# RWKV-7 streaming encoder on one core: pieces, loads and writes around the recurrence moved, and the gate's products around a norm put in a fixed order

## The chip, the cores and the metric

The kernel runs on one core of a Trainium2 chip. A core has a matrix engine (TensorE, PE in the profile; its weight loads are PEld), VectorE (DVE), ScalarE (ACT), GpSimd (POOL) and SyncE (SP), each with an instruction queue of its own that runs in order, and 16 DMA engines. The metric is the device time of one execution in microseconds; the median of the runs counts, lower is better.

## The reference, cut to what matters

A trunk of two residual layers on an input of 1024 tokens by 1024 columns, each followed by a SwiGLU FFN, and a norm at the end. The first layer is a mixer that the change does not touch. The second is RWKV-7 time mixing; its state is a recurrence over the tokens, per head of 64 columns (16 heads):

```python
def step(state, inp):
    r_t, w_t, k_t, v_t, a_t, b_t = inp
    sa = jnp.einsum('bhvk,bhk->bhv', state, a_t)
    state = (state * w_t[:, :, None, :] + sa[..., None] * b_t[:, :, None, :]
             + v_t[..., None] * k_t[:, :, None, :])
    return state, jnp.einsum('bhvk,bhk->bhv', state, r_t)
...
y = ((y - mean) * lax.rsqrt(var + GN_EPS)).reshape(bsz, seq, d)
y = y * ln_w.astype(f32) + ln_b.astype(f32)
bonus = jnp.sum(rh * kh * r_k.astype(f32), axis=-1, keepdims=True) * vh
y = (y + bonus.reshape(bsz, seq, d)).astype(h.dtype)
return (y * g) @ w_o, v_first
```

The gate is `g = sigmoid(xg @ g1) @ g2` with 160 columns between. `rms_norm` stands before each layer and each FFN.

## The kernel before, in words

Tokens are worked in two halves of 512 (half 0, half A; half 1, half B). A product in float32 is made of three products of parts, high by high, high by low, low by high (`mm3`, lines 408 to 411; a dense block of eight `mm3` is 24 matmuls of 128x128 by 128x512). Weights come by DMA issued on ACT's queue into `raw` and are split into `whi` (ACT) and `wlo` (DVE) by `split` (158 to 160). Other DMAs are issued on SP's queue. A scheduler lays out every engine's order when the kernel is compiled, by priority and by its own estimate of times; `tc.high_priority` moves what it holds ahead, `tc.issue_after` puts instructions behind another on their queue, and `tc.manual_schedule` keeps the written order for the engines it names. At run time each queue runs in that order.

The stages that the change touches, in order of time:

- `project(h)` (1202): the projections of the time mixing for one half. The recurrence is done in chunks of 64 tokens; inside a chunk a triangular system is solved with an inverse, which `invert` (1432) forms in 31 steps on DVE, for four pairs of heads at a time. So there are two inverses per half, the first beside the products for v, the second after it; both use the same buffer `xi` (cleared by POOL, line 1437) and `iat` (loaded at 1273 to 1280). At its end an inverse is copied (1450) and written to `xi_d` by three DMAs (1452, 1454).
- `recur(h)` (1469): eight chunks. `load(c)` (1504) loads `ar` (with `bk`), `XT` (the inverse, from `xi_d`) and `uv`. The first loads, then `stream` (the residual stream H of the other half), then chunk 1's loads are written in that order (1738 to 1744). `gram` makes the Gram products of a chunk from `ar`, `flip_bk` transposes, `below` and `below2` complete the inverse with `XT`, `own` and the rest of `burst` (1589) carry the state. Each product of the recurrence is chained behind the last on PE (`ordered`). `drive` interleaves the recurrence with dense FFN products, with the recurrence at high priority.
- `post(jj)` (1671) works on the output of two chunks: loads of `gch` and `vch`, the product with `bon` on POOL (1685), statistics (1690), a power on POOL (`rsqrt`, 1701 and 414), the norm (1703 on), and `turn_out`, which transposes it on PE and writes `y_d`. It is a generator: `between()` (1666) takes its next step at six places of a burst, behind the last DVE instruction of the recurrence's chain. A post is started after an odd burst and runs in the even one that follows; the last one runs after the eighth burst.
- After the recurrence of half 0 its `y` is read from `y_d` and split into `ahi`, `alo` (`open_act`, 481), and `beside(1, ...)` (994) runs the output projection and the first FFN blocks of half A beside `side`, the token mixes of half B, the low-rank products and the gate (`gate`, 1153: 24 matmuls for `g1`, 24 for `g1b`). At step 8 it calls `norm_a` (2033): row sums of squares by four small matmuls (444), `norm_rows` (mean, POOL's power, a diagonal, a broadcast matmul at 457), and `norm_split` (466), which makes `hn` and its parts for the FFN's products.

Buffers are placed by pools as on a stack. Before, the buffer of H for the first recurrence lies where `xi` of `project` lay.

Of the kernel before, what the change touches and what calls it, by code (L numbers as in the profile page):

```python
# [16 lines left out]
P = 128  # L17
# [28 lines left out]
def tile_trunk(  # L46
# [392 lines left out]

    def norm_bcast(acc):  # L440

        st = auxt()
        for j in range(4):
            pe.matmul(st[:, j : j + 1], acc[:, j * P : (j + 1) * P], onesd, start=True, stop=True)
        return norm_rows(st[:, 0:4])

# [16 lines left out]
    def act_tiles(pool_, n=HT):  # L463
        return [pool_.tile([P, KT, n], F32R, tag=t, name=t) for t in ("ahi", "alo")]

# [528 lines left out]
    def beside(h, gen, weights, parts, at=()):  # L994

        side, lowrank, gate = parts
        at = {} if not at else dict([at])
        due, done = 0.0, 0

        def step():  # L1000
            nonlocal done
            next(side, None)
            done += 1

        for i, weight in enumerate(weights):
            if i == LOWRANK_AT[h]:
                while done < KT:
                    step()
                lowrank()
            if i in at:  # L1010
                at[i]()
            if i == GATE_AT[h]:
                while done < 2 * KT:
                    step()
                gate()
            w = 0.0
            while w < weight - 0.001:
                w += next(gen)
                if i >= MIX_AT[h]:
                    due += 1.0  # L1020
                    while due >= 1.0 and (done < 2 * KT or i >= LOWRANK_AT[h]) and (done < 3 * KT or i >= GATE_AT[h]):
                        due -= 1.0
                        step()
        exhaust(gen)
        exhaust(side)
# [87 lines left out]
    def project_gate(h, hn1, kp, xlp, ring):  # L1113
# [38 lines left out]

        def gate():
            for nm, n in (("g1", P), ("g1b", 96)):
                wg = take((nm, h))
                o = mmt()
                dense2(o[:n], *wg, xs, n)
                t = nt.tile([P, HT], F32, tag="nsq", bufs=2, name="gt")
# [273 lines left out]
    def invert(h, p0, iat, tmp):  # L1432
# [18 lines left out]
        to = xi_d[h][p0 : p0 + 4].rearrange("p r c q i x -> (p r c) q i x")  # L1451
        sp.dma_start(to[:, 0, :, 0:64], x2[0:64].rearrange("s i a j -> s i (a j)"))
        for q in range(2):
            sp.dma_start(to[:, q, :, 64 - 32 * q : 96 - 32 * q], x2[64:128, :, 0, :])  # L1454

# [13 lines left out]
    def recur(h, wp, stream, ratio):  # L1469
# [34 lines left out]
        def load(c):  # L1504
            ab = wt("ar", 2, [P, 2, 8, 2, 64])
            sp.dma_start(ab, ab_d[h][c])
            ar, bk = ab[:, 0], ab[:, 1]
            XT = wt("XT", 2, [P, 8, 96])
            for r in range(2):
                sp.dma_start(XT[rows[r]], xi_d[h][:, r ^ (c % 2), c].rearrange("p q i x -> (q i) p x"))  # L1510
            uv = wt("uv", 2, [P, 2, 8, 64])
            vs = v_d[h][c * 64 : c * 64 + 64]
            sp.dma_start(uv[64:128, 0], vs[:, 0])
            loaded[0] = sp.dma_start(uv[0:64, 1], vs[:, 1])
            gt = wt("gt", 2, [P, 8, 2, P])
            C[c] = (ar, bk, uv, gt, XT)

# [71 lines left out]
        def burst(c, bkt, w1):  # L1589
# [53 lines left out]
            if more:  # L1643
                bkt = flip_bk(c + 1)
                if turned or pieces:
                    for _ in pieces.pop():
                        pass
                    turned.pop()()
# [14 lines left out]

        turned, chain, pieces = [], [None], []

        def between():
            if pieces:
                with tc.issue_after(chain[0]):
                    next(pieces[0], None)

        def post(jj):
            ysb = [ypair.pop(0) for _ in range(2)]
            j = h * 4 + jj
# [13 lines left out]
            yield  # L1687
            for r in range(2):
                for p in range(8):
                    dve.bn_stats(out=st[:, r, p, :], in_=ysb[r][:, p, :])  # L1690
                yield
# [8 lines left out]
            dve.tensor_scalar(out=var, in0=var, scalar1=1.0 / 64, scalar2=GN_EPS, op0=ALU.mult, op1=ALU.add)  # L1700
            rsqrt(var)
            yield
            dve.scalar_tensor_tensor(out=mean, in0=mean, scalar=-0.5, in1=var, op0=ALU.mult, op1=ALU.mult)
# [37 lines left out]
        with tc.issue_after(loaded[0].ins):  # L1741
            stream_loaded = stream()
        with tc.issue_after(stream_loaded):
            load(1)
        yield START * ratio
# [8 lines left out]
        for c in range(8):  # L1754
            bkt, w1 = yield from burst(c, bkt, w1)
            yield BURST / 2
            if c % 2 == 1:
                pieces[:] = [post(c // 2)]
                next(pieces[0])
            yield BURST / 2  # L1760
        for _ in pieces[0]:
# [226 lines left out]

    ps_es = open_psum("psm0", MIXED)
    hb_pool, hb_es = open_pool(name="hb1", bufs=1, side="left")  # L1990
    wp, wp_es = open_pool(name="wp0", bufs=1, side="left")
# [8 lines left out]
    y, y_es = open_pool(name="y0", bufs=1, side="left")  # L2000
    ys = open_act(("y", 0), y)
    between.append(with_first(0))
# [29 lines left out]

    def norm_a():
        hnA.extend(norm_split(0, C_FFN + 8, y, n_d[1], norm_bcast(sums)))

    beside(1, blocks(), [1] * 8 + weights_of(G1A[0]), parts, (8, norm_a))
    for e in (f_es, y_es, hb_es, ps_es):
        e.close()
# [72 lines left out]
```

## Time and profile before

| | us |
|---|---|
| median of 3 runs | 2402.95 |
| lowest, highest | 2401.16, 2412.61 |
| the profiled execution | 2407.23 |
| its span, first to last instruction | 2405.5 |
| PE busy in the span | 2319.2 |
| DVE busy | 1464.6 |
| ACT busy | 946.9 |
| POOL busy | 171.2 |

The granted clock of PE over the span was 0.986. The page gives busy time by engine, then the span in 40 slices, then DMA queues, the chain of work that ended last, and the costliest groups. In the page's slices PE stands at 9 tenths or more in nearly all; 8 stands in the first and the last slice and in those that begin at about 960, 1020, 1140 and 1620 us. A row of the timeline gives start, duration, engine, line, operation, the tiles as output<-inputs, shapes, a count, and in brackets the idle time of the engine before it and what ended it. An engine with a q behind its name (SPq, ACTq) is its sequencer, which issues DMAs.

The page's DMA part lists two queues that carry the kernel's transfers: one with 195.33 MB (27.3% of the 16 engines' span) and one with 150.25 MB (20.9%).

### The profile page before, as it was taken

The numbers are of one execution on the slowest core, as the hardware profiler recorded it, in microseconds if no ns is written. First come the engines' busy times: TensorE is split into PE (matmuls) and PEld (weight loads), VectorE is DVE, ScalarE is ACT, GpSimd is POOL, SyncE is SP. The second block draws the span as 40 slices with busy tenths as digits, with TensorE's granted clock in tenths as the row PEclk, the third lists the DMA queues.
The fourth block names the chain that finished last, engine by engine and source line by source line (L and its number), as shares of the span: only waits on it lengthen the run. The fifth ranks groups of instructions, "written<-read, shape, count | busy, mean of one in ns | idle before, by whom it ended". The sixth has DMA issues, their size and how long they took to land.

```text
span 2405.5 us, 37578 instructions
## 1 busy us (share of the span) xinstructions
PE 2319.2 (96%) x15315; PEld 1893.9 (79%) x15315; DVE 1464.6 (61%) x2312; ACT 946.9 (39%) x1467; POOL 171.2 (7%) x195
## 2 busy tenths in 40 slices
PE   8999999999999999889899999998999999999998
PEld 6888888888888788667777777777778788888886
DVE  6445775665568858656768958765664546444443
ACT  6233444444224755323336665423332225222223
POOL 0200000000000022101100022101010001000001
PEclk9999999999999999999999999999999999999999
DMA  5114472334765565775445475776534433433231
GB/s 181 53 49 145 149 198 83 129 99 146 283 226 191 156 173 140 209 218 157 130 135 165 148 199 147 193 222 177 163 89 149 123 88 119 127 96 97 79 114 44
DMA packets 446157, 347.97 MB, mean 145 GB/s; under 512 B 119776, under 2 KB 393312, under 8 KB 443680
## 3 DMA queue, kind: packets, MB, share of 16 engines
q10 hardware_dynamic: 266048, 195.33, 27.3%
q1 hardware_dynamic: 179936, 150.25, 20.9%
q8 instruction: 120, 1.97, 0.4%
q14 instruction: 53, 0.43, 0.1%
HBM read 266.47 MB, written 79.04 MB: 144 GB/s over the span
## 4 chain that ended last, share of the span: by engine, by line
PE 77%; DVE 9%; DMA 6%; issue 2%; ACT 2%; SPq 2%; POOL 2%; ACTq 0%; POOLq 0%; DVEq 0%
PE mm L409 17%; PE mm L410 17%; PE mm L411 17%; PE mm L740 5%; PE mm L742 5%; PE mm L741 5%; PE sm L1491 3%; DMA ar<-ab_d 1%; DVE wlo L160 1%; DMA raw<-y_d 1%; SPq L1454 1%; DVE it L1443 1%; DMA raw<-in_ffn_w_down_dram 1%; PE mm L590 1%; PE mm L591 1%
## 5 line engine op out<-in xcount | busy, mean ns | idle before, releaser
L409 PE MATMUL mm<-ahi,whi 128*128 128x512 f32 x1376 | 541.0, 394 | 4.2 <-ACT ahi L159 2.6
L410 PE MATMUL mm<-alo,whi 128*128 128x512 f32 x1376 | 542.0, 394 | 0.9 <-DVE alo L160 0.9
L411 PE MATMUL mm<-ahi,wlo 128*128 128x512 f32 x1376 | 540.6, 393 | 1.6 <-DVE wlo L160 1.6
L159 ACT ACTIVATE whi<-raw 128x1024 fp32r<-128x1024 f32 (+2 forms) x284 | 286.3, 1014 | 507.1 <-PE mm L410 367.7
L160 DVE TENSOR_TENSOR wlo<-raw,whi 128x1024 fp32r<-128x1024 f32 (+2 forms) x284 | 337.6, 1192 | 233.6 <-ACT whi L159 212.4
L409 PEld LDWEIGHTS mm<-ahi,whi 128*128 128x128 f32 x1376 | 259.0, 188 | 62.9 <-issue 3.5
L411 PEld LDWEIGHTS mm<-ahi,wlo 128*128 128x128 f32 x1376 | 259.2, 188 | 58.5 <-DVE wlo L160 2.9
L410 PEld LDWEIGHTS mm<-alo,whi 128*128 128x128 f32 x1376 | 259.3, 188 | 57.4 <-issue 2.9
L503 DVE TENSOR_TENSOR h<-h,mm 128x512 f32<-128x512 f32 x276 | 185.9, 684 | 156.1 <-PE mm L411 152.9
L411 PE MATMUL mm<-hidhi,wdlo 128*128 128x512 f32 x304 | 119.6, 394 | 0.0
L409 PE MATMUL mm<-hidhi,wdhi 128*128 128x512 f32 x304 | 117.2, 392 | 2.3 <-ACT sg L957 2.3
L410 PE MATMUL mm<-hidlo,wdhi 128*128 128x512 f32 x304 | 118.6, 390 | 0.0
L740 PE MATMUL mm<-ahi,whi 128*128 128x512 f32 x296 | 115.6, 390 | 0.0
L741 PE MATMUL mm<-alo,whi 128*128 128x512 f32 x296 | 115.2, 389 | 0.0
L742 PE MATMUL mm<-ahi,wlo 128*128 128x512 f32 x296 | 113.6, 389 | 0.0
L965 DVE TENSOR_TENSOR sg<-sg,mm 128x512 f32<-128x512 f32 x52 | 35.7, 686 | 125.7 <-PE mm L411 125.7
L159 ACT ACTIVATE wdhi<-raw 128x1024 fp32r<-128x1024 f32 x42 | 43.6, 1058 | 169.0 <-PE mm L410 126.9
L160 DVE TENSOR_TENSOR wdlo<-raw,wdhi 128x1024 fp32r<-128x1024 f32 x42 | 51.4, 1223 | 30.9 <-ACT wdhi L159 29.2
L409 PEld LDWEIGHTS mm<-hidhi,wdhi 128*128 128x128 f32 x304 | 57.2, 188 | 14.7 <-ACT sg L957 2.7
L411 PEld LDWEIGHTS mm<-hidhi,wdlo 128*128 128x128 f32 x304 | 57.2, 188 | 12.2 <-issue 0.5
L410 PEld LDWEIGHTS mm<-hidlo,wdhi 128*128 128x128 f32 x304 | 57.2, 188 | 12.0 <-issue 0.2
L409 PE MATMUL mm<-xhi,whi 128*128 128x512 f32 (+1 forms) x160 | 64.9, 406 | 0.0
(392 smaller groups left out, 4226.2 us busy)
## 6 DMA issues: line engine op xcount, KB each, us to landing
raw<-in_ffn_w_down_dram ACTq DMA_DIRECT2D x88, 512.0 KB
raw<-in_ffn_w_gate_dram ACTq DMA_DIRECT2D x74, 512.0 KB
raw<-in_ffn_w_up_dram ACTq DMA_DIRECT2D x74, 512.0 KB
hid_d<-hid SPq DMA_DIRECT2D x36, 512.0 KB
ar<-ab_d SPq DMA_DIRECT2D x16, 1024.0 KB
hd<-hid_d SPq DMA_DIRECT2D x26, 512.0 KB
raw<-in_ab_w_in_dram ACTq DMA_DIRECT2D x16, 512.0 KB
raw<-in_ab_w_out_dram ACTq DMA_DIRECT2D x16, 512.0 KB
```

Source lines behind the costliest of these rows:

```text
L159: act.activation(hi, src, AF.Copy)
L160: (eng or dve).tensor_tensor(out=lo, in0=src, in1=hi.bitcast(F32), op=ALU.subtract)
L409: pe.matmul(o, whi, xhi, start=first, stop=False)
L410: pe.matmul(o, whi, xlo, start=False, stop=False)
L411: newest[0] = pe.matmul(o, wlo, xhi, start=False, stop=last).ins
L503: dve.tensor_tensor(out=H[h][:, m, :], in0=H[h][:, m, :], in1=o, op=ALU.add)
L590: pe.matmul(ops[j], xhi[:, k, sl], whi[:, kk], start=(k == 0), stop=False)
L740: pe.matmul(o, wh[:, k, :], x[0][:, k, :], start=st, stop=False, skip_group_check=True)
L741: pe.matmul(o, wh[:, k, :], x[1][:, k, :], start=False, stop=False, skip_group_check=True)
L742: pe.matmul(o, wl[:, k, :], x[0][:, k, :], start=False, stop=k == 3, skip_group_check=True)
L965: dve.tensor_tensor(out=s, in0=s, in1=o, op=ALU.mult)
L1491: i = f(*args, **kw)
```

## The change

Six things are done.

1. `row_sums` is split from `norm_bcast`. `norm_a` now gets the gate from `beside` and runs it in a fixed order on PE: the 24 products of `g1`, the row sums, 12 products of `g1b`, the broadcast, the other 12. `norm_rows` and `norm_split` stand at high priority.
2. The three writes of an inverse are issued by POOL and not by SP.
3. `load_x` loads `XT` by itself: for chunk 0 behind the stream of H and ahead of chunk 1's loads, else with the chunk as before. `XT` is allocated after `gt`.
4. A `post` is started before the odd burst, with its loads; in the odd burst one step of it is taken (`open_`), the rest in the even burst. It takes a chunk's output from `ypair` only when it needs it.
5. Behind the power of `post` one more `yield` stands, so that one place of a burst lies between it and the instruction that reads it.
6. `ahi` of half 0's `y` has a pool of its own, `yhi`, opened ahead of H's buffer.

```diff
@@ -437,12 +437,16 @@
 
         return acc, add
 
-    def norm_bcast(acc):
+    def row_sums(acc):
 
         st = auxt()
         for j in range(4):
             pe.matmul(st[:, j : j + 1], acc[:, j * P : (j + 1) * P], onesd, start=True, stop=True)
-        return norm_rows(st[:, 0:4])
+        return st[:, 0:4]
+
+    def norm_bcast(acc):
+
+        return norm_rows(row_sums(acc))
 
     def norm_rows(ms, scale=1.0):
 
@@ -461,7 +465,7 @@
         return norm_bcast(norm_sums(h))
 
     def act_tiles(pool_, n=HT):
-        return [pool_.tile([P, KT, n], F32R, tag=t, name=t) for t in ("ahi", "alo")]
+        return [(pool_[i] if type(pool_) is tuple else pool_).tile([P, KT, n], F32R, tag=t, name=t) for i, t in enumerate(("ahi", "alo"))]
 
     def norm_split(h, c0, pool_, spill=None, b=None):
 
@@ -1007,12 +1011,13 @@
                 while done < KT:
                     step()
                 lowrank()
-            if i in at:
-                at[i]()
             if i == GATE_AT[h]:
                 while done < 2 * KT:
                     step()
-                gate()
+                if i in at:
+                    at[i](gate)
+                else:
+                    gate()
             w = 0.0
             while w < weight - 0.001:
                 w += next(gen)
@@ -1150,11 +1155,11 @@
 
         xs = []
 
-        def gate():
+        def gate(between=()):
             for nm, n in (("g1", P), ("g1b", 96)):
                 wg = take((nm, h))
                 o = mmt()
-                dense2(o[:n], *wg, xs, n)
+                dense2(o[:n], *wg, xs, n, between if nm == "g1b" else ())
                 t = nt.tile([P, HT], F32, tag="nsq", bufs=2, name="gt")
                 act.activation(t[:n], o[:n], AF.Tanh, scale=0.5)
                 sigm(t[:n], t[:n])
@@ -1449,9 +1454,9 @@
             yield
         dve.tensor_copy(x2[:, :, 0, :], xi.rearrange("p i c -> p c i"))
         to = xi_d[h][p0 : p0 + 4].rearrange("p r c q i x -> (p r c) q i x")
-        sp.dma_start(to[:, 0, :, 0:64], x2[0:64].rearrange("s i a j -> s i (a j)"))
+        pool.dma_start(to[:, 0, :, 0:64], x2[0:64].rearrange("s i a j -> s i (a j)"))
         for q in range(2):
-            sp.dma_start(to[:, q, :, 64 - 32 * q : 96 - 32 * q], x2[64:128, :, 0, :])
+            pool.dma_start(to[:, q, :, 64 - 32 * q : 96 - 32 * q], x2[64:128, :, 0, :])
 
 
 
@@ -1505,15 +1510,17 @@
             ab = wt("ar", 2, [P, 2, 8, 2, 64])
             sp.dma_start(ab, ab_d[h][c])
             ar, bk = ab[:, 0], ab[:, 1]
-            XT = wt("XT", 2, [P, 8, 96])
-            for r in range(2):
-                sp.dma_start(XT[rows[r]], xi_d[h][:, r ^ (c % 2), c].rearrange("p q i x -> (q i) p x"))
             uv = wt("uv", 2, [P, 2, 8, 64])
             vs = v_d[h][c * 64 : c * 64 + 64]
             sp.dma_start(uv[64:128, 0], vs[:, 0])
             loaded[0] = sp.dma_start(uv[0:64, 1], vs[:, 1])
-            gt = wt("gt", 2, [P, 8, 2, P])
-            C[c] = (ar, bk, uv, gt, XT)
+            C[c] = (ar, bk, uv, wt("gt", 2, [P, 8, 2, P]), wt("XT", 2, [P, 8, 96]))
+            if c:
+                load_x(c)
+
+        def load_x(c):
+            for r in range(2):
+                loaded[0] = sp.dma_start(C[c][4][rows[r]], xi_d[h][:, r ^ (c % 2), c].rearrange("p q i x -> (q i) p x"))
 
         def gram(c, q):
             ar, bk, _, gt, _ = C[c]
@@ -1642,9 +1649,8 @@
             yield 0.1
             if more:
                 bkt = flip_bk(c + 1)
-                if turned or pieces:
-                    for _ in pieces.pop():
-                        pass
+                if c and c % 2 == 0:
+                    exhaust(pieces.pop())
                     turned.pop()()
                 if c < 6:
                     load(c + 2)
@@ -1661,15 +1667,16 @@
                 yield 0.1
             return bkt, w1
 
-        turned, chain, pieces = [], [None], []
+        turned, chain, pieces, open_ = [], [None], [], [0]
 
         def between():
-            if pieces:
+            if pieces and open_[0]:
+                open_[0] -= 1
                 with tc.issue_after(chain[0]):
                     next(pieces[0], None)
 
         def post(jj):
-            ysb = [ypair.pop(0) for _ in range(2)]
+            ysb = []
             j = h * 4 + jj
             gch = wt("gch", 1, [P, 8, P])
             vch = wt("vch", 1, [P, 2, 8, 64])
@@ -1686,6 +1693,7 @@
             st = wt("st", 1, [P, 2, 8, 6])
             yield
             for r in range(2):
+                ysb.append(ypair.pop(0))
                 for p in range(8):
                     dve.bn_stats(out=st[:, r, p, :], in_=ysb[r][:, p, :])
                 yield
@@ -1699,6 +1707,7 @@
             dve.tensor_tensor(out=var, in0=var, in1=dm, op=ALU.add)
             dve.tensor_scalar(out=var, in0=var, scalar1=1.0 / 64, scalar2=GN_EPS, op0=ALU.mult, op1=ALU.add)
             rsqrt(var)
+            yield
             yield
             dve.scalar_tensor_tensor(out=mean, in0=mean, scalar=-0.5, in1=var, op0=ALU.mult, op1=ALU.mult)
             vb, mb = (bc(t[:, 0:8].unsqueeze(2), [P, 8, 64]) for t in (var, mean))
@@ -1741,6 +1750,8 @@
         with tc.issue_after(loaded[0].ins):
             stream_loaded = stream()
         with tc.issue_after(stream_loaded):
+            load_x(0)
+        with tc.issue_after(loaded[0].ins):
             load(1)
         yield START * ratio
         last.append(newest[0])
@@ -1752,12 +1763,12 @@
         w1 = below(0)
         yield 2.0
         for c in range(8):
-            bkt, w1 = yield from burst(c, bkt, w1)
-            yield BURST / 2
             if c % 2 == 1:
                 pieces[:] = [post(c // 2)]
                 next(pieces[0])
-            yield BURST / 2
+            open_[0] = (99, 1)[c % 2]
+            bkt, w1 = yield from burst(c, bkt, w1)
+            yield BURST
         for _ in pieces[0]:
             yield 0.3
         turned.pop()()
@@ -1987,6 +1998,7 @@
 
 
     ps_es = open_psum("psm0", MIXED)
+    yhi, yhi_es = open_pool(name="y0hi", bufs=1, side="left")
     hb_pool, hb_es = open_pool(name="hb1", bufs=1, side="left")
     wp, wp_es = open_pool(name="wp0", bufs=1, side="left")
     f, f_es = open_pool(name="ffn1", bufs=1, side="right")
@@ -1998,7 +2010,7 @@
     drive(ffn(0, 1, nxt["hn"], f, D0P[:3], nd=2), recur(0, wp, in_pieces(hb_pool, 1, h_d[1, 0]), 6.2), 6.2)
     wp_es.close()
     y, y_es = open_pool(name="y0", bufs=1, side="left")
-    ys = open_act(("y", 0), y)
+    ys = open_act(("y", 0), (yhi, y))
     between.append(with_first(0))
     drive(ffn(0, 1, nxt["hn"], f, D0P[3:], nd=2))
     drive(steps_b)
@@ -2030,11 +2042,23 @@
         yield from out_proj(0, ys, sums_a)
         yield from ffn(1, 0, hnA, f, G1A[0], nd=2, after=spill_a)
 
-    def norm_a():
-        hnA.extend(norm_split(0, C_FFN + 8, y, n_d[1], norm_bcast(sums)))
+    def norm_a(gate):
+        got = []
+        between = [lambda: None] * KT
+        between[0] = lambda: got.append(row_sums(sums))
+
+        def rows_():
+            with tc.high_priority(offset=AHEAD):
+                got.append(norm_rows(got[0]))
+
+        between[4] = rows_
+        with tc.manual_schedule(engines={mybir.EngineType.PE}):
+            gate(between)
+        with tc.high_priority(offset=AHEAD):
+            hnA.extend(norm_split(0, C_FFN + 8, (yhi, y), n_d[1], got[1]))
 
     beside(1, blocks(), [1] * 8 + weights_of(G1A[0]), parts, (8, norm_a))
-    for e in (f_es, y_es, hb_es, ps_es):
+    for e in (f_es, y_es, hb_es, yhi_es, ps_es):
         e.close()
     ps_es = open_psum("psp1", PROJ)
     project(1, hn1, kp, ring, keep, early("n1", "act2", nxt["a_es"]))
```

## The prediction, made before the result

> **What bounds the kernel.** I read the page first, then the windows (busy time by stretch), then the timeline of single engines where the windows show TensorE (PE) idle.
>
> ```profile
> PE 2319.2 (96%) x15315; PEld 1893.9 (79%) x15315; DVE 1464.6 (61%) x2312; ACT 946.9 (39%) x1467; POOL 171.2 (7%) x195
> ```
>
> PE is busy for 2319.2 of 2405.5 us. At most 86.3 us of idle time can go, and what a halved clock costs after it. The change takes out no product that weighs, so the question is which of these idle stretches it touches.
>
> ```profile
> core 0: us, PE busy (x) PEld busy (x) DVE busy (x) ACT busy (x) POOL busy (x), PEclk, DMA share, GB/s
> 960.00:1040.00 80.00, 72.09 (x344) 57.61 (x343) 59.44 (x119) 32.27 (x46) 8.27 (x4) 1.00 0.68 185
> 1040.00:1060.00 20.00, 9.97 (x214) 8.42 (x212) 5.77 (x10) 2.01 (x6) 0.00 (x0) 0.74 1.03 290
> 1080.00:1240.00 160.00, 149.66 (x2485) 119.72 (x2484) 106.90 (x247) 54.24 (x108) 20.18 (x8) 0.97 0.47 140
> 1600.00:1620.00 20.00, 17.54 (x302) 14.10 (x305) 8.39 (x14) 2.60 (x6) 0.00 (x0) 0.91 0.92 285
> 1640.00:1660.00 20.00, 16.12 (x314) 13.12 (x308) 12.46 (x33) 6.73 (x12) 1.90 (x1) 0.91 0.50 141
> 1660.00:1740.00 80.00, 76.78 (x1380) 61.73 (x1376) 53.29 (x112) 27.69 (x57) 10.59 (x4) 1.00 0.58 165
> 1740.00:1760.00 20.00, 17.20 (x326) 13.66 (x326) 16.49 (x47) 8.89 (x18) 2.90 (x1) 0.91 0.31 87
> ```
>
> Ten of 20 us are idle where the first recurrence starts (1040 to 1060), and the clock stands at 0.74 there. The first recurrence (1080 to 1240) loses 160 - 149.66 = 10.3 us, the second (1640 to 1760) 3.9 + 3.2 + 2.8 = 9.9 us. Those are the places that the change works on, with the stretch around 1335 (below).
>
> **The start of a recurrence.** What held PE at 1042.9 is read in SP's queue:
>
> ```profile
> 1035.34 1.09 DVE L1450 COPY xi<-xi 128x1024 f32<-128x1024 f32 x1
> 1036.50 0.61 SPq L1452 DMA_DIRECT2D xi_d<-xi  x1
> 1037.16 7.18 SPq L1454 DMA_DIRECT2D xi_d<-xi  x2
> 1044.43 2.68 SPq L1506 DMA_DIRECT2D ar<-ab_d  x1
> 1048.93 1.27 SPq L1510 DMA_DIRECT2D XT<-xi_d  x2
> 1052.41 3.69 PE L1491 MATMUL sm<-ar 64*64 64x128 f32 x64 [9.50 <-DMA ar<-ab_d]
> 1056.03 1.51 PE L1491 MATMUL sm<-ident,ar 128*128 128x128 f32 x8
> 1057.46 0.45 PE L1491 MATMUL sm<-XT,gt 32*32 32x32 f32 x32
> ```
>
> The load of `ar` stands behind the three writes of the inverse, though it reads nothing of them; its Gram products stand at the head of PE's queue and hold everything behind. The change sends the writes to POOL's queue and puts the loads of `XT` behind the stream of H, so `ar` can be issued as soon as SP is done with the last rows of v. The 9.50 us go. What is late next is `XT`, for the products `below`. From the end of the copy (1035.34 + 1.09 = 1036.43) to the issue of the `XT` load (1048.93) the writes took 12.5 us; for the load's landing I take 4 us (between 0 and the 8.5 us from 1048.93 to 1057.46). PE, starting its Gram products at 1042.9, comes to `below` after 3.69 + 1.51 us, at 1048.1. So it waits until 1052.9, 4.8 us: the gain is 9.5 - 4.8 = **4.7 us**, and the half clock stays. Behind the waiting `XT` load on SP stand the loads of chunk 1; they were issued at about this time before, so I put no price on them.
>
> The second half in the same way:
>
> ```profile
> 1584.38 1.09 DVE L1450 COPY xi<-xi 128x1024 f32<-128x1024 f32 x1
> 1597.20 1.27 SPq L1510 DMA_DIRECT2D XT<-xi_d  x2
> 1602.32 3.04 PE L1491 MATMUL sm<-ar 64*64 64x128 f32 x64 [2.67 <-DMA ar<-ab_d]
> 1610.34 0.45 PE L1491 MATMUL sm<-XT,gt 32*32 32x32 f32 x32
> ```
>
> Here the writes took 1597.20 - 1585.47 = 11.7 us; with 4 us for the load `XT` is there at 1601.2, and `below` would stand at 1610.34 - 2.67 = 1607.7. No wait takes the place: **2.7 us**, and half of what the clock of 0.91 over 20 us costs (1.8 us), **0.9**.
>
> **The writes on POOL.** No transfer in this trace is issued by POOL, so their price is unknown. The low end is SP's 12.5 us, less the queue. The high end comes from how far POOL is stretched beside other work:
>
> ```profile
> 912.04 0.74 POOL L1374 TENSOR_SCALAR ar<-kkn 128x8 f32<-128x8 f32 x1 [0.96 <-ACT kkn L1369]
> 961.89 4.16 POOL L1374 TENSOR_SCALAR ar<-kkn 128x8 f32<-128x8 f32 x1 [3.20 <-ACT kkn L1369]
> ```
>
> The same instruction takes 0.74 or 4.16 us, 5.6 times as long. Against SP's issue of 7.84 us (1036.50 to 1044.34) that is 44 us, and with the 4.6 us from there to 1048.93 some 49 us. I take SP's 12.5 us: the same packets go through the same 16 DMA engines, and it is the only row of these transfers.
>
> The Trainium skill, page "SBUF — State Buffer", section "SBUF: two separate sides", speaks against this edit: descriptors of a transfer issued by GpSimd are written by GpSimd's own cores, and these are locked out while VectorE runs an operation that takes both ports; it names 620 ns that became 3100 ns. By that factor of five the writes would take 62 us as an estimate, and the sum below would end near 2481 us. No run here shows such a transfer yet; the two rows of POOL agree in kind.
>
> The first inverse of each half is moved too:
>
> ```profile
> 979.89 11.28 SPq L1454 DMA_DIRECT2D xi_d<-xi  x2
> 991.27 2.42 SPq L1274 DMA_DIRECT2D iat<-at_d  x1
> 998.85 1.82 POOL L1437 MEMSET xi<- 128x2048 f32 x1 [30.89 <-DMA v_d<-sg]
> 999.85 1.32 DVE L1281 TENSOR_SCALAR iat<-iat 128x32 f32<-128x32 f32 x1 [4.03 <-DMA iat<-n_d]
> ```
>
> The second load of `iat` no longer stands 11.28 us behind the writes. But the second inverse also needs the buffer `xi`, which is free only when the writes have read it (the clearing at 998.85), so I put this at nothing. On POOL the clearing stands behind the writes; it waits for them anyway, and POOL has no other work from 968 to 998.85.
>
> **The pieces beside the recurrence.** `post` starts one burst earlier (loads, the product with `bon`, half of the statistics), and there is an empty step behind POOL's power, whose result VectorE (DVE) now asks for one step later.
>
> ```profile
> L414 POOL TENSOR_TENSOR var<-var,small x8: 2899/2902/3871, 1104.1 to 1788.5; 128x16 f32<-128x16 f32 x8
>   POOL var L414: 6.2, 4
> 1194.01 0.18 DVE L1703 SCALAR_TENSOR_TENSOR mean<-mean,var 128x16 f32<-128x16 f32 x1 [2.38 <-POOL var L414]
> 1196.30 0.66 PE L1491 MATMUL sm<-ident,ar 128*128 128x128 f32 x4 [1.94 <-DVE gt L1530]
> 1198.18 0.45 PE L1491 MATMUL sm<-ident,ysb 128*128 128x128 f32 x1 [1.23 <-DVE ysb L1714]
> ```
>
> The power takes 2.9 us; line 1703, which reads it, kept DVE idle for 6.2 us in 4 cases (second line: what line 1703 waited for). In the case shown DVE's 2.38 us cost PE 1.94 + 1.23 us, so I take PE's gain as large as DVE's: **6.2 us**. The bounds are 0 (PE has dense products beside it) and the 20.2 us of both recurrences. Of the clock (0.97 over 160 us and 0.91 over 20 us: 4.8 + 1.8 us) I take a quarter, **1.6 us**. The last piece of each half is shorter by its loads and half its statistics; in half 0 its end leads to the loads of `y_d`, where I take **1 us**. The loads of `gch` and `vch` now stand ahead of chunk c+2's on SP; those have a whole chunk of slack.
>
> `ahi` of `y` gets its own place (`yhi`), which moves H's buffer off that of the inverse: the stream need not wait for the writes. It is what lets `XT` stand behind the stream at no price.
>
> **The second norm of half A.**
>
> ```profile
> 1326.69 0.69 DVE L2025 TENSOR_TENSOR nacc<-nacc,nsq 128x512 f32<-128x512 f32 x1
> 1328.45 0.39 PE L411 MATMUL mm<-xhi,wlo 128*128 128x512 f32 x1
> 1332.13 0.95 PE L444 MATMUL aux<-small,nacc 128*128 128x1 f32 x8
> 1335.67 1.10 PE L457 MATMUL aux<-ndg,ones 128*128 128x512 f32 x2 [0.44 <-DVE ndg L453]
> 1339.39 0.97 PE L409 MATMUL mm<-ahi,whi 128*128 128x512 f32 x3 [2.62 <-ACT ahi L159]
> 1341.25 0.79 PE L410 MATMUL mm<-alo,whi 128*128 128x512 f32 x1 [0.90 <-DVE alo L160]
> ```
>
> The gate's 24th product starts at 1328.45; the row sums came behind the 39th (1332.13), the broadcast behind the 48th (1335.67), and PE then stood for 2.62 and 0.90 us. The sums are ready at 1327.4, so row sums at 1328.7 need not wait. From row sums to broadcast it took 3.5 us; 12 products of 0.23 us and the sums fill 3.6. So the broadcast comes at 1332.3, 3.4 us earlier, and the other 12 products lie beside `hn` and `ahi` (3.7 us from broadcast to first product). I take **3.3 us** and nothing of the clock, since DVE's pace over the eight blocks (0.7 us each for `hn` and for `alo`) then sets it. If `nacc` comes late in the new order, PE waits for it with everything behind: that would cost at most what is gained.
>
> **Sum.** 4.7 + 3.6 + 7.8 + 1.0 + 3.3 = 20.4 us. Against it stands that the compiler lays out all queues anew, and a dense stretch can then meet a late weight. At 1640 to 1660 PE loses 3.9 us, as much as I take off: **4 us**. So 16.4 us from the profiled execution's 2407.23 us: 2390.8. The median shown (2402.95) is 4.3 us under it: **2387 us**, 0.7% faster.
>
> **Rivals.** A measurement of this kernel tells some 0.5%, 12 us, from no change.
>
> *POOL writes slowly (slower).* One mechanism: `XT` comes late at `below(0)`, and PE stands with the dense products behind it. With t for the writes the waits are t - 7.7 us (half 0, before 9.5) and t - 18.2 us (half 1, before 2.7). At t = 30, between the ends, 22.3 + 11.8 - 12.2 = 21.9 us are lost, less the 8 that the other parts leave (7.8 + 1.0 + 3.3 - 4): 2417 us. It decides from t of 23 us on, where the sum is zero. For it: POOL's stretched row, and DVE busy in the same stretch (59.44 of 80 us). Against it: dense products can be laid ahead of `below`. At 49 us it would be 2455.
>
> *Another wait takes each place (same).* DVE is the engine behind many waits, and its work stays the same; the time saved at one chunk is waited for at the next, and only norm and second start remain, 6.9 us: 2396 us. Against it: the waits named here end on POOL and SP, not on DVE's load.
>
> *All goes (faster still).* The compiler lays dense products ahead of `below`, the clock stays full at the starts (0.26 and 0.09 of 20 us, 7 us), and the recurrences lose half their 20.2 us: beyond the forecast 4.8 at the start, 6 of clock, 2 in the recurrences and the 4 of the new order: 2370 us.
>
> **Chances.** Forecast 0.45 (2379 to 2395, two thirds of it over 0.5%: 0.31 faster, 0.14 same), slow POOL 0.21, same 0.19, all goes 0.15. Faster 0.46, same 0.33, slower 0.21. The forecast's own range is 2379 to 2395. The range of 8 in 10 is 2368 to 2416: it takes in "same", most of "all goes", and slow POOL as far as t = 29.
>
> **What would show it.** Half 0: PE's Gram products follow the dense ones without the 9.50 us, and the wait stands at the first product with `XT`, about 5 us. The transfers on POOL: under 13 us from the copy to the `XT` load, and their issue in POOL's rows. Line 1703 no longer waits for POOL. The first product with the new `ahi` stands within 1 us of the gate's last. Wrong would be: over 23 us for the writes; a wait of PE at `XT` in half 1; DVE's order with the clearing of `xi` at its head while weights are late.

## The result, and the profile after

| | before | after |
|---|---|---|
| median of 13 runs | 2404.07 us | 2391.27 us |
| lowest, highest | 2396.93, 2412.61 | 2381.56, 2397.57 |
| the profiled execution | 2407.23 | 2386.18 |
| its span | 2405.5 | 2384.4 |
| PE idle in the span | 86.3 | 69.2 |

The ratio after to before is 0.9948, 95% interval 0.9934 to 0.9963: 12.5 us, 0.52% faster, against a forecast of 2387 us. The two profiled executions lie further apart (21 us) than the medians. One run of e3 below took 3845.79 us at a granted clock of 0.555; it stands in that row's median and not in its ratio. The rows below are of the profile after, whose line numbers are those of before plus 4 to 13.

The timeline at the start of the first recurrence (the last two rows: of the second):

```profile
1025.01 1.08 DVE L1455 COPY xi<-xi 128x1024 f32<-128x1024 f32 x1
1026.63 1.09 POOL L1457 DMA_DIRECT2D xi_d<-xi  x1 [37.19 <-DVE xi L1455]
1027.71 2.17 POOL L1459 DMA_DIRECT2D xi_d<-xi  x2
1036.90 1.98 PE L1496 MATMUL sm<-ar 64*64 64x128 f32 x64
1039.56 0.32 SPq L1853 DMA_DIRECT2D h<-h_d  x1
1041.04 1.29 SPq L1523 DMA_DIRECT2D XT<-xi_d  x2
1045.98 0.45 PE L1496 MATMUL sm<-XT,gt 32*32 32x32 f32 x32 [2.36 <-DMA XT<-xi_d]
1588.05 1.98 PE L1496 MATMUL sm<-ar 64*64 64x128 f32 x64
1598.60 0.45 PE L1496 MATMUL sm<-XT,gt 32*32 32x32 f32 x32
```

The Gram products (1036.90) have no bracket: the 9.50 us are gone. The wait stands at `XT`, with 2.36 us; the load of `XT` was issued 15.0 us after the end of the copy (1026.09 to 1041.04), behind the last load of the stream. In the second half neither product waits. POOL's issue of the three writes took 3.3 us.

The line that reads POOL's power, by source:

```profile
L1712 DVE SCALAR_TENSOR_TENSOR mean<-mean,var x8: 171/175/177, 1096.3 to 1777.8; 128x16 f32<-128x16 f32 x8
its engine sat idle before it (us, times) until:
  POOL var L414: 1.1, 1
```

Before it was 6.2 us in 4 cases. So far all went as meant. The loss is new, and it stands where the first recurrence ends, at the output projection:

```profile
1241.81 0.79 PE L409 MATMUL mm<-ahi,whi 128*128 128x512 f32 x1 [8.89 <-ACT ahi L159]
1253.97 0.50 PE L409 MATMUL mm<-ahi,whi 128*128 128x512 f32 x1 [0.77 <-ACT whi L159]
1257.92 0.79 PE L411 MATMUL mm<-ahi,wlo 128*128 128x512 f32 x1 [3.22 <-DVE wlo L160]
```

```profile
core 0: us, PE busy (x) PEld busy (x) DVE busy (x) ACT busy (x) POOL busy (x), PEclk, DMA share, GB/s
1220.00:1270.00 50.00, 36.58 (x138) 28.40 (x137) 41.60 (x65) 26.00 (x42) 1.20 (x2) 0.80 0.66 200
1270.00:1320.00 50.00, 49.36 (x219) 39.78 (x219) 39.00 (x55) 33.47 (x50) 2.53 (x2) 1.00 0.38 103
```

The windows say that PE is idle for 13.4 of the first 50 us, and that the clock stands at 0.80. That makes 20 us at half clock, but not 10 us of loss, since PE stood still in part of them. The rows tell how much was worked slowly: a dense product is 0.63 us long from 1241.81 to 1248.80 and from 1257.92 to 1262.35, and 0.39 us in between, as in this pair:

```profile
1244.96 0.63 PE L409 MATMUL mm<-ahi,whi 128*128 128x512 f32 x1
1249.64 0.39 PE L409 MATMUL mm<-ahi,whi 128*128 128x512 f32 x1
```

The slow stretches are 11.4 us long, so at half clock some 6 us were lost. In the profile before, the window from 1220 has:

```profile
1220.00:1270.00 50.00, 46.45 (x255) 36.24 (x253) 34.83 (x63) 17.76 (x27) 3.34 (x2) 1.00 0.44 144
```

Why, can be counted. The windows of line 409 alone (a third of the dense products) from the first Gram product to the last product of the recurrence, and from there to the first output projection, first before, then after:

```profile
1052.40:1225.70 173.30, 47.53 (x115) 0.96 0.56 162
1225.70:1263.90 38.20, 18.65 (x47) 1.00 0.42 137
```

```profile
1036.90:1210.10 173.20, 54.08 (x132) 0.99 0.58 164
1210.10:1241.80 31.70, 12.02 (x30) 0.90 0.41 136
```

The recurrence takes as long as it did, but three times 17 dense products more lie in it, 11.6 us at 0.227 each (the spacing of their rows): that is the idle time that was saved. They are missing behind it. `y` needs some 30 us from the last product to `ahi` (24 before), and the 90 products there cover 20.4 of them; before there were 141 (32 us). A part of the way has grown too: the write of `y_d`, first before, then after, comes 16.6 us behind the last product (1225.7), and now 21.7 us (1210.1).

```profile
1242.28 0.53 SPq L1734 DMA_DIRECT2D y_d<-gch  x1
1231.76 0.54 SPq L1743 DMA_DIRECT2D y_d<-gch  x1
```

The next table adds up the two profiled executions.

| stretch of the profiled execution | before | after | difference |
|---|---|---|---|
| to the first Gram product | 1052.4 | 1036.9 | -15.5 |
| to the last product of the first recurrence | 173.3 | 173.2 | -0.1 |
| to the first output projection | 38.2 | 31.7 | -6.5 |
| to the first product with the new `ahi` | 75.5 | 83.3 | +7.8 |
| to the end of the span | 1066.1 | 1059.3 | -6.8 |

From the first Gram product to the first product with the new `ahi` it is 287.0 us before and 288.2 after, with the same 774 dense products: in half 0 all that the recurrence saved was given back at its end. What remains lies ahead of the first Gram product and in half 1.

Some 5 of the 15.5 us are not the change's: the profile before has a stop of 1.75 us at 863.08, in a stretch that the change leaves as it was, where the clock is 0.89 from 840 to 870. The profile after has neither, and of the later runs e2, e5 and e9 have the stop again (2.23, 1.58 and 2.66 us).

At the second norm of half A, the timeline of PE and DVE:

```profile
1314.12 0.95 PE L444 MATMUL aux<-small,nacc 128*128 128x1 f32 x8
1318.56 1.10 PE L461 MATMUL aux<-ndg,ones 128*128 128x512 f32 x2 [0.64 <-DVE ndg L457]
1318.94 0.68 DVE L160 TENSOR_TENSOR glo<-gt,ghi 128x512 fp32r<-128x512 f32 x1
1319.54 0.68 DVE L1187 TENSOR_TENSOR alo<-mix,ahi 128x512 fp32r<-128x512 f32 x1
1320.14 1.62 DVE L1194 SCALAR_TENSOR_TENSOR mix<-hn,vec,mix 128x512 f32<-128x512 f32 x2
1321.68 0.68 DVE L1187 TENSOR_TENSOR xlo<-mix,xhi 128x512 fp32r<-128x512 f32 x1
1322.28 0.74 DVE L477 SCALAR_TENSOR_TENSOR hn<-h,vec,aux 128x512 f32<-128x512 f32 x1
1325.10 0.97 PE L409 MATMUL mm<-ahi,whi 128*128 128x512 f32 x3 [2.67 <-ACT ahi L159]
1331.06 0.80 PE L410 MATMUL mm<-alo,whi 128*128 128x512 f32 x1 [1.68 <-DVE alo L160]
```

The broadcast (1318.56) does come in the middle of the gate, but `hn`, which needs it, stands on DVE behind the token mixes until 1322.28. PE waits 2.67 us, as before the change (2.62).

### The profile page after: what moved, and what is told of

The parts are those of the page before. It is cut to its first block, busy times and chain, and to the rows that moved or that the text cites. A ratio compares the mean times of both kernels' runs of the same rounds, so it can differ in the third digit from the quotient of the medians.

```text
span 2384.4 us, 37572 instructions
## 1 busy us (share of the span) xinstructions
PE 2315.2 (97%) x15315; PEld 1892.5 (79%) x15315; DVE 1465.3 (61%) x2312; ACT 947.4 (40%) x1467; POOL 182.5 (8%) x207
## 4 chain that ended last, share of the span: by engine, by line
PE 83%; DVE 7%; DMA 4%; ACT 2%; issue 2%; POOL 1%; SPq 0%; ACTq 0%; POOLq 0%; DVEq 0%
PE mm L409 19%; PE mm L411 19%; PE mm L410 19%; PE mm L744 5%; PE mm L746 5%; PE mm L745 5%; PE sm L1496 4%; DVE wlo L160 1%; DMA raw<-y_d 1%; DVE it L1448 1%; PE yp L1496 1%; PE aux L1420 1%; PE aux L1421 1%; PE mm L594 1%; PE aux L1422 1%
## 5 line engine op out<-in xcount | busy, mean ns | idle before, releaser
L409 PE MATMUL mm<-ahi,whi 128*128 128x512 f32 x1376 | 542.5, 397 | 12.8 <-ACT ahi L159 11.9
L409 PEld LDWEIGHTS mm<-ahi,whi 128*128 128x128 f32 x1376 | 260.0, 189 | 71.6 <-ACT ahi L159 13.2
L410 PEld LDWEIGHTS mm<-hidlo,wdhi 128*128 128x128 f32 x304 | 57.4, 189 | 11.9
L744 PEld LDWEIGHTS mm<-ahi,whi 128*128 128x128 f32 x296 | 55.6, 188 | 11.7 <-issue 0.2
```

The source lines that it names most:

```text
L409: pe.matmul(o, whi, xhi, start=first, stop=False)
L410: pe.matmul(o, whi, xlo, start=False, stop=False)
L744: pe.matmul(o, wh[:, k, :], x[0][:, k, :], start=st, stop=False, skip_group_check=True)
```

## The experiments

The third column is the ratio to before, the last the difference to the changed kernel from the two ratios; such a difference is known to some 5 us. Each edit also makes the compiler lay out the queues anew: e7, which takes out one `yield`, has 371 dense products in the first recurrence where the changed kernel has 396. So an undone part is priced together with its order.

| run | median, us | ratio to before, 95% interval | to the changed kernel, us |
|---|---|---|---|
| changed kernel | 2391.27 | 0.9948 (0.9934 to 0.9963) | |
| e1, writes back on SP | 2406.38 | 1.0018 (1.0005 to 1.0032) | +17 |
| e2, post as before | 2400.53 | 0.9995 (0.9978 to 1.0012) | +11 |
| e3, norm as before | 2393.33 | 0.9955 (0.9938 to 0.9973) | +2 |
| e4, two down blocks moved | 2391.19 | 0.9955 (0.9938 to 0.9971) | +2 |
| e5, before and POOL writes | 2404.26 | 1.0013 (0.9998 to 1.0029) | +16 |
| e6, load order as before | 2394.45 | 0.9959 (0.9946 to 0.9973) | +3 |
| e7, one yield | 2410.58 | 1.0034 (1.0018 to 1.0050) | +21 |
| e8, one down block, three slots | 2380.12 | 0.9912 (0.9894 to 0.9930) | -9 |
| e9, before and post | 2397.72 | 0.9984 (0.9967 to 1.0001) | +9 |
| e10, before, POOL writes and post | 2393.29 | 0.9962 (0.9945 to 0.9978) | +3 |
| e11, e8 with the norm as before | 2388.30 | 0.9944 (0.9923 to 0.9965) | -1 |
| e12, before with e8's block | 2414.14 | 1.0041 (1.0027 to 1.0055) | +22 |

**e1.** The changed kernel with

```diff
-        pool.dma_start(to[:, 0, :, 0:64], ...)
+        sp.dma_start(to[:, 0, :, 0:64], ...)
...
-            pool.dma_start(to[:, q, ...], x2[64:128, :, 0, :])
+            sp.dma_start(to[:, q, ...], x2[64:128, :, 0, :])
```

> The changed kernel with the three writes of each inverse back on SP's queue; all else as changed. Theory A (the queue was what mattered): ar stands behind the writes again, so the Gram products of half 0 come some 8 to 10 us later and the second load of iat stands behind 11 us of writes; 8 to 14 us slower than the changed kernel's 2391, so 2399 to 2405. Theory B (the order of the loads did it, XT behind the stream of H): within 3 us of 2391.

It was 17 us slower, more than theory A's 8 to 14. SP's queue and PE in its timeline:

```profile
1030.67 6.72 SPq L1459 DMA_DIRECT2D xi_d<-xi  x2
1037.51 2.92 SPq L1511 DMA_DIRECT2D ar<-ab_d  x1
1046.36 3.69 PE L1496 MATMUL sm<-ar 64*64 64x128 f32 x64 [9.06 <-DMA ar<-ab_d]
```

The 9 us are back, so the queue, not the order of the loads, held `ar`. They are not the whole price. At the first product with the new `ahi` this profile is only 4.2 us behind the changed kernel's (1329.3 against 1325.1), since PE's stops at the output projection are smaller (2.84 us for H, then 0.85 for `y`). The other 14 of the 18 us between the two profiles come later, with stops of 3.69 us for `ar` at 1597.97 and of 6.34 us for DVE at 1641.76 among them.

**e5.** The kernel before with the same three lines turned to `pool`, nothing else.

> The kernel before with one part of the change: the three writes of each inverse on POOL's queue. With the writes back on SP the changed kernel was 16 us slower, with the post pieces as before 11 us slower, which is more together than the 12.5 us that the whole change gains. Theory A (the parts add, and something else in the change costs some 15 us): about 16 us faster than before, 2386 to 2390. Theory B (a part alone gains little, since the first half's PE order then has 90 products behind the recurrence in place of 141, and what is gained at its start is waited for at the output projection): within 5 us of before, 2397 to 2407, with the 9.5 us ahead of the Gram products gone and an idle time of 8 us or more ahead of the output projection.

Nothing was gained, as theory B had it. The 9.5 us are gone here too, but PE stops at two new places in half 0, both in its timeline:

```profile
1026.11 1.08 DVE L1450 COPY xi<-xi 128x1024 f32<-128x1024 f32 x1
1038.86 2.01 SPq L1510 DMA_DIRECT2D XT<-xi_d  x2
1042.29 1.95 SPq L1842 DMA_DIRECT2D h<-h_d  x4
1047.10 0.79 PE L409 MATMUL mm<-hidhi,whi 128*128 128x512 f32 x1 [5.95 <-DVE h L503]
1253.93 0.80 PE L409 MATMUL mm<-ahi,whi 128*128 128x512 f32 x1 [8.64 <-ACT ahi L159]
```

The load of `XT` waits on SP for the writes, the stream of H stands behind it, and PE stands 5.95 us for the residual addition; and at the output projection 8.64 us appear, much like the changed kernel's 8.89. The two do not make up the whole: at the first product with the new `ahi` this profile is still 9.0 us ahead of before's (1330.4 against 1339.4). That is lost in half 1, where H is waited for again (3.02 us at 1602.72) and the second recurrence takes 192.1 us in place of 183.1, from its first Gram product to its last product. The rows above also give the clean price of the writes, since here nothing but they hold the `XT` load: from 1027.19 (end of the copy) to 1038.86, 11.7 us; in half 1 it is 12.7 (1580.04 to 1592.71).

**e6.** The changed kernel with `XT` loaded ahead of the stream again.

```diff
-            if c:
-                load_x(c)
+            load_x(c)
...
-            load_x(0)
-        with tc.issue_after(loaded[0].ins):
             load(1)
```

> The changed kernel with the loads of XT at their old place (for chunk 0 ahead of the stream of H, within the chunk's loads). Theory A (XT's load waits for the writes of the inverse on POOL, and the stream of H behind it on SP comes some 10 us later, but PE asks for H later still): within 3 us of 2391. Theory B (H comes late and the first residual additions, and with them PE's banks, wait): 4 to 12 us slower.

3 us slower, less than the two ratios can tell from nothing: by the time, theory A. But its trace has the mechanism of B: PE stands 4.97 us for H ahead of a row at 1049.9, and 8.80 us for `y`. `XT` is loaded 11.6 us after the copy here (15.0 in the changed kernel), and PE has no stop at it. So the order of the loads takes out the stop for H and puts one at `XT` in its place; how much of it reaches the end was not settled.

**e2, e7, e9: the pieces.** e2 undoes parts 4 and 5 of the change, e9 does them alone on the kernel before, and e7 is the changed kernel with

```diff
             rsqrt(var)
             yield
-            yield
```

> The changed kernel with the post pieces as before (started behind the odd burst, no second yield behind the power). Theory A (the cover behind the recurrence is short): as in the changed kernel 90 dense products stand behind the last product of half 0's recurrence, so the idle time ahead of the first output projection stays at 6 to 9 us, the waits of the mean's line for POOL come back (about 6 us in 4 cases), and the kernel is 4 to 8 us slower than 2391. Theory B (the new pieces made the way from the last product to y_d longer, 16.3 to 21.4 us): that way is 16 us again, the idle time falls to 4 us or less, and the kernel is within 2 us of 2391 or faster.

> The changed kernel with one yield behind the power of post in place of two. 115 dense products stand behind the last product of the first recurrence in place of 90. Prediction's step: VectorE waits for POOL's power again, 4 to 6 us slower than 2391. Rival (the 25 products more are cover, 5.7 us): the idle time at the output projection falls from 8.9 to about 3 us, its half clock goes too, and the kernel is 0 to 6 us faster.

> The kernel before with the new post pieces alone (start before the odd burst, second yield). Theory A (each part pays by itself): 9 to 11 us faster than before, 2391 to 2394, as the run with the post pieces undone says. Theory B (post and writes pay only together, since what the one gains in the recurrence the other's wait at its start takes away): within 4 us of before's 2402, with the 9.5 us ahead of the Gram products still there.

e2 was slower by 11 us, in the direction of theory A and more than its 4 to 8; DVE waited 12.9 us for POOL in 6 cases. PE's stop at the output projection stayed (8.69 us), and the way from the last product to the write of `y_d` was 21.7 us in both, so the new pieces did not lengthen it; with them alone (e9) it was 15.7. e9 gained 4 us, with an interval that touches zero, nearer to theory B; the 9.52 us ahead of the Gram products were still there. e7 was the surprise: 21 us slower, worse than the old pieces. Its rows, the line of the power and the line of ACT's `uv` by source, then one case on ACT and PE:

```profile
L1711 DVE SCALAR_TENSOR_TENSOR mean<-mean,var x8: 165/174/178, 1093.2 to 1794.6; 128x16 f32<-128x16 f32 x8
...
  POOL var L414: 8.6, 5
...
  ACT ysb L1714: 34.0, 8
```

```profile
L1618 ACT ACTIVATE uv<-sm x16: 572/590/593, 1058.2 to 1781.9; 64x512 f32<-64x512 f32 x16
...
  PEld sm L1496: 21.0, 10
```

```profile
1657.07 2.76 ACT L1714 ACTIVATE ysb<-ysb,mean,var 128x64 f32<-128x64 f32 x8 [5.50 <-DVE mean L1711]
1659.74 0.58 ACT L1618 ACTIVATE uv<-sm 64x512 f32<-64x512 f32 x1
1660.37 0.33 PE L1496 MATMUL sm<-uv,bkt 128*64 128x64 f32 x2 [2.84 <-ACT uv L1618]
```

DVE's wait for POOL is only 8.6 us. But ACT has eight activations that need the result, 2.76 us, and behind them in its queue stands the copy of `uv`, on which the recurrence and PE depend. By the code, of the six places of a burst the third lies ahead of that copy and the fourth behind it. With the early start and one yield the norm falls on the third; the second yield moves it to the fourth, where the old pieces had it. PE's weight loads waited 21.0 us for `uv` here, and 3.0 us in the changed kernel; PE's six longest stops for `uv` sum to 16.6 us.

**e10.** Parts 2 and 4, 5 on the kernel before.

> The kernel before with two parts of the change, the writes on POOL and the new post pieces; XT's loads, y's place and the norm as before. Theory A (these two carry the change): 2388 to 2395. Theory B (the load of XT behind the stream of H is needed too, since PE stood 5.95 us for H in the run with the writes alone): 2396 to 2403.

0.9962 against 0.9948: the two carry most of the change. The runs are not additive: alone they give +0.13% and -0.16%, together -0.38%. PE's stop for `y` (8.84 us) is that of the changed kernel; that for H (5.36 us) comes on top, where the changed kernel has the one at `XT`.

**e4, e8, e12: the cover.** Down blocks of the FFN of half 1 are moved from the stage beside the token mixes of half 0 to behind the first recurrence. e4 moves two, e8 one, with three slots for the hidden blocks in place of two; e12 is e8's edit on the kernel before. e8 in short (the three-block sets used for `third` are picked by length):

```diff
-    D0B = [[a, a + 1, a + 2] for a in range(f, f + 12, 3)], [[a, a + 1] for a in range(f + 12, 22, 2)]
+    D0B = [[a, a + 1, a + 2] for a in (f, f + 3, f + 6)] + [[f + 9, f + 10]], [[19, 20], [21]]
...
-    _, hslot = slots_of(f, 0, 2)
+    _, hslot = slots_of(f, 0, 3)
```

> The changed kernel with two of the FFN's down blocks of half 1 (48 dense products, 10.9 us) moved from the stage beside the token mixes of half 0 to the stretch behind the first recurrence: 152 products stand behind its last product in place of 90. Theory A (the gain was given back because y comes 31.7 us after the last product and 90 products cover 20.4 us of it): the 8.9, 0.8 and 3.2 us of idle time at the output projection go, with some 8 us of half clock; up to 6 us are lost where the blocks were taken; 2371 to 2382. Theory B (PE would wait there for the weights of the output projection or for y in any case): within 4 us of 2391.

> The changed kernel with one down block of half 1 (24 products, 5.4 us) moved behind the first recurrence, and three slots for the hidden blocks there in place of two, so that no load of them is late (in the run with two blocks moved, 3.1 us were). 139 products stand behind the last product of the recurrence in place of 90. Theory A (y's way from the last product to the output projection, 31.7 us, is what PE waits for): the idle time there goes, no new one comes, 2377 to 2385. Theory B (what is saved there is waited for later, where VectorE has the token mixes and the norm of half A to do): within 4 us of 2391.

> The kernel before with the down block moved and three slots, as in the faster version, and nothing else of the change. The order then has 102 dense products behind the first recurrence's last product (before 141, although 24 more are there in all). Theory A (the block pays only where the recurrence has been shortened): 2398 to 2408. Theory B (the move pays by itself): 8 to 12 us faster than before, 2391 to 2395.

e4 took as long as the changed kernel, which is theory B's time. The stop for `y` went, but others came; its timeline has, behind the recurrence:

```profile
1223.34 0.50 PE L409 MATMUL mm<-hd,whi 128*128 128x512 f32 x1 [1.63 <-DVE h L507]
1233.53 0.47 PE L409 MATMUL mm<-hd,whi 128*128 128x512 f32 x1 [3.09 <-DMA hd<-hid_d]
```

By the code, with two slots a hidden block could not be loaded until the pair ahead of it was done. e8, one block and three slots, is the fastest kernel of this study, 0.9912 of before. Its windows:

```profile
1220.00:1270.00 50.00, 45.73 (x195) 35.85 (x194) 35.40 (x51) 18.59 (x24) 2.16 (x2) 0.97 0.60 183
1270.00:1320.00 50.00, 46.27 (x196) 36.05 (x194) 46.68 (x69) 37.41 (x59) 2.53 (x2) 0.97 0.42 120
```

PE is idle for 4.3 of 50 us where it was for 13.4, at a clock of 0.97, and there is no stop for `y`. From the last product to the first with the new `ahi` it takes 118.0 us (115.0 in the changed kernel) with 49 dense products, 11.1 us, more in it. From 1270 on PE loses 3.7 us where the changed kernel lost 0.6, with DVE busy for 46.68 of 50 us and a stop of 2.07 us for DVE's `h` at 1275.99: part of what was saved is waited for at DVE, which has the token mixes to do. e12 was 22 us slower than the changed kernel and 0.41% slower than before: `ar` still held PE (6.40 us), and the compiler's new order left 102 products behind the recurrence, fewer than the 141 of before, with a stop of 4.23 us for `y`. It is slower than either theory had it, and the block does not pay by itself.

**e3, e11: the norm.** Part 1 undone in the changed kernel and in e8.

> The changed kernel with the second norm of half A and the gate in the order of before (row sums and broadcast where the scheduler puts them). The prediction's step: 3.3 us slower than 2391. Theory A (the earlier broadcast was given back, since hn and ahi come later on VectorE and ScalarE): within 2 us of 2391, with PE idle ahead of the first product with the new ahi for 2 to 4 us.

> The version with one down block moved and three slots, with the second norm of half A and the gate as before. The prediction's step: 3.3 us slower than that version's 2380. Theory A (the norm part gains nothing, since hn stands behind six other instructions on VectorE): within 2 us of 2380.

e3 is equal to the changed kernel by its time, which is too coarse to exclude 3.3 us by itself. e11 is 8 us slower than e8, with intervals that just touch. On the spot neither trace shows a gain: from the last product of the first recurrence to the first with the new `ahi` it is 115.0 us (changed) against 112.5 (e3), and 118.0 (e8) against 118.1 (e11). Of the 6 us between the profiles of e8 and e11, 4.3 lie ahead of the norm (last product at 1203.6 and 1207.9), where their code is the same. What makes up e11's 8 us stays open.

## Why the prediction was right in the sum, and where its steps were wrong

The time came out 4 us above the forecast, by gains and a loss that were both larger than forecast. That the two left nearly the forecast sum is luck.

- **Start of half 0 (4.7 us).** Right in mechanism: the 9.50 us went, and a wait at `XT` took their place, 2.36 us in place of 4.8, since 16 dense products lie between the Gram products and `XT`. The half clock, which the step left standing, went for the Gram products (1.98 us in place of 3.69). That the load of `XT` stands behind the stream at no price was not borne out: it was issued 15.0 us after the copy, not under 13, and PE waited for it; in e5 and e6, ahead of the stream, it took 11.7 and 11.6. What the place avoids is a stop for H, 5.95 and 4.97 us there.
- **Start of half 1 (2.7 and 0.9).** Right: no wait at either product.
- **Writes on POOL (12.5 us, bounds to 49).** The taken value was right: 11.7 and 12.7 us in e5, against 12.5 and 11.7 on SP. The rival of slow writes fell. The factor of five that the Trainium skill names on its page "SBUF — State Buffer", section "SBUF: two separate sides", did not show, though DVE was busy for 59.0 of the 80 us from 960 to 1040. While POOL issued the second inverse's writes (1026.63 to 1029.87), DVE ran only TENSOR_TENSOR, and no run here tells whether that takes both ports. What the edit saved was SP's queue, which these three writes had held for 7.8 us before. This agrees with the page "DMA: Bandwidth & Descriptors" of the Trainium skill, section "Issuing engines are not separate DMA queues", by which another issuing engine saves the sequencer's time alone.
- **The first inverse (nothing).** Too low by a little: from the first copy to the second it took 50.9 us, 57.6 before and 53.8 in e1, so 2.9 us are the queue's in half 0; the other 3.8 went in e1 too, without the writes on POOL.
- **Pieces beside the recurrence (7.8 us).** Right in size (11 us undone, 4 alone, each some 5 us uncertain), but the mechanism reaches further than the step had it. It counted DVE's wait for POOL. e7 shows that the early start alone would have cost, through ACT's queue, more than the old pieces did.
- **Tail of half 0 (1 us).** Right for the pieces alone, wrong in the new order. From the last product to the write of `y_d` it was 16.6 us before, 15.7 with the pieces alone (e9) and 21.7 after. By e2, with 21.7 too, the loss isn't the pieces'. In the trace after DVE makes residual additions of the down blocks (`h<-h,mm`) between the steps of the last post from 1212 on, in the trace before none until 1242. Over the runs the way grows with the number of these additions in it: one (before, e9) 15.7 and 16.6 us, eight or nine (e1, e4, e7, e8, e11) 18.1 to 20.8, thirteen (the changed kernel, e2, e3, e5, e6, e10, e12) 20.8 to 21.8. This fits dense work that stands further along; it was not tried by itself.
- **Second norm (3.3 us).** This step failed. "The other 12 products lie beside `hn` and `ahi` (3.7 us from broadcast to first product)" took over a duration from an order in which `hn` came 2.3 us after the broadcast (1337.93 against 1335.67). In the new order it comes 3.7 us after it, and its `ahi` then stands on ACT behind a weight's split, the gate's tanh and a mix (until 1324.43). The way from broadcast to first product is 6.5 us, and the products only cover what this adds. The first new product came 2.67 us after the gate, not within 1.
- **New order (4 us against).** The largest mis-size: 13.4 us idle and some 6 of half clock at the output projection, where 3.6 and none stood before. The rival "another wait takes each place" had the right kind of mechanism, with `y` in the place of DVE.
- **The clock.** The rival "all goes" priced a clock of 0.74 over 20 us at 5.2 us. But PE was busy for only 9.97 of these 20, and in the trace for 4.5 us of the half clock: some 2 us were lost.
- **The sum itself.** It added parts priced one by one. Undone singly, writes and pieces cost 17 and 11 us, more than the whole gain of 12.5; done singly they gain nothing that can be told from zero.

Shown is that PE waits for `y` at the output projection and that cover removes the wait (e8). Part 6 was undone in no run by itself. Not shown is why the compiler's order has some 395 products in the first recurrence in e1 and e5, which hold only one of the two queue edits each, and 345 before.

## What to carry to other kernels

A chain that runs beside filler work has two ends: making it faster also uses the filler up earlier, so count the filler that is left behind the chain's last product against the way from there to its consumer, before adding up the waits that go. A wait of one engine is priced by what is queued behind its dependents, not by its own length: 8.6 us of waits for POOL cost some 20 us through eight activations ahead of one copy. Price a low clock only where the engine works. And undo parts singly and do them singly; where the two disagree, the parts may share a bound.

## What was not expected of the hardware

Three writes of an inverse took 3.3 us of POOL's issue where SP's queue had been held for 7.8 and 11.9 us by those of half 0, and the load that depends on them was issued after about the same time (11.7 and 12.7 us in e5, 12.5 and 11.7 before). A power on POOL of 128x4 elements took 1.93 us in the changed kernel's norm and 1.45 before. Stops of PE of 8.89 and 3.22 us were followed by 7.0 and 4.4 us in which a dense product took 0.63 us in place of 0.39, so that the clock added some 6 us to 12 of stops.
